# Prompt attention in a hybrid decoder step: keys of the preceding block copied over masked keys, values summed in column halves

## The chip, the cores and the metric

The kernel runs on one core of a Trainium2 chip. The metric is the device time of one execution in microseconds (us). The engines are TensorE (PE in the profile; PEld is its weight loads), VectorE (DVE), ScalarE (ACT), GpSimd (POOL) and SyncE (SP, which only issues DMAs here).

## The reference

One inference step of a two-layer decoder trunk, for a prompt (16 meta tokens and 256 prompt tokens, 272 columns) and a sample group (8 sequences of 4 tokens, 32 columns): 304 columns in all. Per layer:

```
proj = x @ w_in                       # q (8 heads x 64), k, v (2 groups x 64), xr, gate, g_attn, g_lru
attn = sliding-window attention (window 128, rotary, a learned sink per head)
rec  = RG-LRU(causal_conv(xr)) * gelu(gate)
mix  = (sigmoid(g_attn) * attn @ w_attn_proj + sigmoid(g_lru) * rec @ w_lru_proj) @ w_out
x = LayerNorm(alpha * x + mix);  x = LayerNorm(alpha * x + SwiGLU(x))
```

The prompt's attention, which the change touches, is

```
valid = (kp <= qp) & (kp > qp - 128) & (kp >= 0)      # kp, qp: positions of key and query
s = where(valid, q @ k.T / 8, -1e30);  m = max(s.max(), sink)
p = exp(s - m);  out = (p / (p.sum() + exp(sink - m))) @ v
```

So a query sees itself and the 127 positions before it. Prompt queries are cut into block 0 (the 16 meta tokens), block 1 and block 2 (128 each). For query i of a block of 128, the valid keys are keys 0 to i of its own block and keys i+1 to 127 of the block that precedes: always 128 places, one for each index.

## The kernel before, in words

Activations lie transposed, features on the partitions and the 304 tokens in the columns. Each fp32 weight block of 128x1024 is loaded by SyncE, copied by ScalarE to a rounded part (`wh`, line 212) and reduced by VectorE to the remainder (`wl`, line 213) in `prep`; every product is three matmuls in the rounded format (`product`, lines 363 to 365). `ahead` keeps these preparations `LA` = 4 units ahead of TensorE, over `WB` = 5 buffers. A product over a whole input is 24 matmuls and is called a step here.

Per layer: the grouped products for k, v and the first two q (lines 415 to 419), rotary, and then a list of steps (xr, ga, gate, gl), between which smaller work is hung by a plan written by hand (`PLAN`, `BEHIND`, lines 35 to 44): the turning of values (`v_turn`), the attention units, the convolutions, the LRU gates (lines 700 to 711) and the recurrence. Then come the attention projection, the LRU projection, the output projection with a norm and the SwiGLU.

An attention unit (`Unit`) is a pair of heads per group for one block of queries; layer 0 has one unit of block 0 and two each of blocks 1 and 2, layer 1 the latter four. Both have one `Sample` unit for the sample group. A unit has three stages:

- `scores`: a bf16 matmul of the identity with the mask (line 516) puts 0 or -8e30 in a PSUM bank, for each group; four fp32 products of K = 64 rows are added (line 521), on 144 key columns in block 1 and 256 in block 2. VectorE takes the maximum (line 527), ScalarE the exponentials with their sums (line 534), VectorE normalizes (line 540).
- `turn`: TensorE transposes the probabilities (lines 554 and, for the 16 meta keys, 558) and ScalarE copies them from PSUM (lines 560 and 563).
- `values`: products of 256 columns with the values (line 574), over value tiles that are padded with zeros so that each group writes its half of the 128 output partitions and all are added in one bank: three in block 1, four in block 2. `split` (lines 350 and 351) makes the two parts for the projection.

`BEHIND` sets how many steps lie between a unit's stages: in layer 0 turning comes three steps after scores and values one step after turning, in layer 1 four and three. The tiles of SBUF come from a pool of `SLOTS` buffers. Except in two blocks that fix an order, the framework's planner orders the instructions of each engine by the program's order and its own estimates of time, and sets the semaphores; an engine runs its list in order.

Of the kernel before, what the change touches and what calls it, by code (L numbers as in the profile page):

```python
# [122 lines left out]
def trunk_kernel(ctx, tc, I, O):  # L123
# [132 lines left out]
    mask1 = const("mask1", [128, 144], BF)  # L256
    mask2 = const("mask2", [128, 256], BF)
    mask0 = const("mask0", [16, 16], BF)
# [26 lines left out]
    dve.memset(eps, EPS)  # L285
    qblk = consts.tile([128, NB, 2, 4, NS], F32, name="qblk")
# [137 lines left out]
    for l in range(DEPTH):  # L424
# [9 lines left out]
        vt = slot(nm("vt"), [128, T])  # L434
        vz = slot(nm("vz"), [128, 2, 2, 128])
        v0 = slot(nm("v0"), [128, 2, 128])
        pool.memset(vz, 0.0)
        pool.memset(v0[:, 0], 0.0)
# [33 lines left out]
        def evac_v(ps):  # L472
            if fold is None:
                act.activation(vt, ps[:, :T], AF.Copy)
            else:
                unfold(ps, T, allc, vt)

        def v_turn():
            p = bank(nm("vT"))
            p3 = p.rearrange("p (a b) -> p a b", a=4)  # L480
            for j, (a, b) in enumerate(((0, 16), (16, 144), (144, 272), (272, 304))):
                pe.transpose(p3[:b - a, j, :], vt[:, a:b], identf)
            for g in range(2):
                d = slice(64 * g, 64 * g + 64)
                act.activation(vz[:, :, g, d], p3[:, 1:3, d], AF.Copy)
                act.activation(v0[32 * g:32 * g + 16, 0, d], p3[:16, 0, d], AF.Copy)
                pool.dma_start(O["wvp"][l][:, d], vz[:, 1, g, d])
            act.activation(v0[:32, 1, :], p3[:32, 3, :], AF.Copy)
            pool.dma_start(O["wvn"][l], v0[:32, 1, :])
# [4 lines left out]
        VN = v0[:, 1, :]  # L494
        BLK = {
            0: dict(q0=0, nq=16, keys=(0, 16), mask=mask0, first=True, v=()),
            1: dict(q0=16, nq=128, keys=(0, 144), mask=mask1, first=True, v=(0,)),
            2: dict(q0=144, nq=128, keys=(16, 272), mask=mask2, first=False, v=(0, 1)),
        }

        class Unit:

# [4 lines left out]
            def __init__(self, b, ts):  # L507
                self.B, self.ts, self.nt = BLK[b], ts, len(ts)

            def scores(self):  # L510
                B, nt = self.B, self.nt
                nq, (k0, k1) = B["nq"], B["keys"]
                nk = k1 - k0
# [12 lines left out]
                for g in range(2):  # L526
                    dve.tensor_reduce(mx[:, g], p3[g], axis=AX.X, op=OP.max)
# [595 lines left out]
```

## Time and profile before

| | us |
|---|---|
| median of 3 runs | 925.61 (922.74 to 925.91) |
| the profiled execution | 924.32 |
| its span, first to last instruction | 922.6 |
| TensorE busy | 891.0 |
| VectorE busy | 700.5 |
| ScalarE busy | 504.2 |
| GpSimd busy | 185.4 |

Times in the profile are those of the one profiled execution. Matmul ends are modelled and matmuls overlap, so the price of one is best read from the start of the next or from the chain of work that ended last, which gives to each step only the time by which it delays the next. An fp32 matmul has two records, one in bf16 or in the rounded format has one, and a transpose has one. The granted clock of TensorE is given as a share: 1.00 is 2.4 GHz, 0.50 is 1.2 GHz.

### The profile page before, as it was taken

The page shows a single profiled execution, that of the slowest core. Times are in us where ns is not written, and L with a number is a line of the kernel's source. Part 1 is how long each engine was busy: PE and PEld are TensorE (multiplying, and loading weights), DVE is VectorE, ACT ScalarE, POOL GpSimd, SP SyncE. Part 2 cuts the span into 40 slices and gives each one's busy share as a digit, 9 for nine tenths or more (in the row PEclk, how much of TensorE's full clock was granted, in tenths as well). Part 3 has the DMA queues.
Part 4 walks back from the last instruction along what each step waited for, and adds up shares of the span by engine and source line. Part 5 has one row for each costly group of instructions (what it writes and reads, how often), then busy time and mean ns, then how long its engine had stood idle before and what let it go on. Part 6 is the DMA issues. An engine that isn't in the chain of part 4 may idle for free.

```text
span 922.6 us, 16033 instructions
## 1 busy us (share of the span) xinstructions
PE 891.0 (97%) x6414; PEld 870.9 (94%) x6414; DVE 700.5 (76%) x1169; ACT 504.2 (55%) x876; POOL 185.4 (20%) x253
## 2 busy tenths in 40 slices
PE   7998999999999999999997999999999999999993
PEld 6987899999999999999997998999999999999993
DVE  5676859567998667677899888795689975877865
ACT  4864794444665334444557877963456643434432
POOL 2930219012300000000262431040252000000025
PEclk9998999999999999999998999999999999999997
DMA  7753135535345443554455253155444454445401
GB/s 247 278 193 120 53 131 184 183 138 180 140 138 180 140 161 115 185 180 138 142 213 167 91 190 112 72 181 187 163 157 152 168 175 150 144 172 183 168 16 52
DMA packets 26411, 141.61 MB, mean 153 GB/s; under 512 B 3336, under 2 KB 7464, under 8 KB 12000
## 3 DMA queue, kind: packets, MB, share of 16 engines
q1 hardware_dynamic: 25280, 137.93, 43.7%
q0 software_dynamic: 1056, 2.66, 0.9%
q8 instruction: 50, 0.82, 0.4%
q14 instruction: 25, 0.20, 0.1%
HBM read 136.74 MB, written 3.83 MB: 152 GB/s over the span
## 4 chain that ended last, share of the span: by engine, by line
PE 83%; DVE 4%; ACT 2%; issue 1%; POOL 0%; DVEq 0%; ACTq 0%
PE f L364 10%; PE f L363 10%; PE f L365 10%; PE rs L365 7%; PE rs L363 7%; PE rs L364 7%; PE gate L363 2%; PE gl L363 2%; PE rp L363 2%; PE gate L364 2%; PE rp L365 2%; PE gl L364 2%; PE rp L364 2%; PE gate L365 2%; PE gl L365 2%; PE o L574 1%
## 5 line engine op out<-in xcount | busy, mean ns | idle before, releaser
L212 ACT ACTIVATE wh<-raw 128x1024 fp32r<-128x1024 f32 (+2 forms) x255 | 263.1, 1034 | 237.1 <-PE rs L365 66.4
L213 DVE TENSOR_TENSOR wl<-raw,wh 128x1024 fp32r<-128x1024 f32 (+2 forms) x255 | 310.7, 1222 | 85.3 <-ACT wh L212 82.9
L364 PE MATMUL f<-dh,wl 128*128 128x306 f32 (+1 forms) x640 | 192.4, 301 | 0.0
L363 PE MATMUL f<-dh,wh 128*128 128x306 f32 (+1 forms) x640 | 192.2, 300 | 0.0
L365 PE MATMUL f<-dl,wh 128*128 128x306 f32 (+1 forms) x640 | 192.0, 300 | 0.0
L365 PEld LDWEIGHTS f<-dl,wh 128*128 128x128 f32 x640 | 120.7, 189 | 0.0
L364 PEld LDWEIGHTS f<-dh,wl 128*128 128x128 f32 x640 | 120.7, 189 | 0.0
L363 PEld LDWEIGHTS f<-dh,wh 128*128 128x128 f32 x640 | 120.6, 188 | 0.0
L363 PE MATMUL rs<-fh,wh 128*128 128x304 f32 (+1 forms) x352 | 105.4, 300 | 0.0
L364 PE MATMUL rs<-fh,wl 128*128 128x304 f32 (+1 forms) x352 | 104.9, 299 | 0.0
L365 PE MATMUL rs<-fl,wh 128*128 128x304 f32 (+1 forms) x352 | 104.9, 299 | 0.0
L913 POOL TENSOR_TENSOR acc<-acc,X 128x304 f32<-128x304 f32 (+1 forms) x23 | 29.7, 1290 | 359.1 <-ACT e L908 195.1
L363 PEld LDWEIGHTS rs<-fh,wh 128*128 128x128 f32 x352 | 66.3, 188 | 0.5 <-ACT fh L350 0.2
L364 PEld LDWEIGHTS rs<-fh,wl 128*128 128x128 f32 x352 | 66.2, 188 | 0.1
L365 PEld LDWEIGHTS rs<-fl,wh 128*128 128x128 f32 x352 | 66.1, 188 | 0.0
L864 DVE TENSOR_TENSOR X<-X,rs 128x304 f32<-128x304 f32 (+1 forms) x64 | 29.4, 459 | 32.2 <-PE rs L365 31.7
L363 PE MATMUL xr<-xh,wh 128*128 128x304 f32 x128 | 40.8, 319 | 4.9 <-ACT xh L791 3.9
L960 DVE SCALAR_TENSOR_TENSOR u<-c,c,f 128x304 f32<-128x304 f32 (+1 forms) x80 | 41.4, 520 | 1.8
L959 DVE COPY c<-f 128x2 f32<-128x2 f32 x80 | 12.5, 158 | 39.3 <-PE f L365 39.1
L365 PE MATMUL xr<-xl,wh 128*128 128x304 f32 x128 | 39.6, 312 | 1.6 <-DVE xl L793 1.6
L364 PE MATMUL xr<-xh,wl 128*128 128x304 f32 x128 | 39.5, 312 | 0.0
L363 PE MATMUL gate<-xh,wh 128*128 128x304 f32 (+1 forms) x128 | 39.2, 306 | 0.0
(307 smaller groups left out, 2226.1 us busy)
## 6 DMA issues: line engine op xcount, KB each, us to landing
raw<-in_wts SPq DMA_DIRECT2D x112, 1024.0 KB, 4.9
raw<-in_wts SPq DMA_DIRECT2D x16, 768.0 KB, 4.3
raw<-in_wts SPq DMA_DIRECT2D x3, 512.0 KB, 9.0
kc<-in_kcache SPq DMA_DIRECT2D x4, 256.0 KB, 7.1
vc<-in_vcache SPq DMA_DIRECT2D x4, 256.0 KB, 7.1
out_wks<-kc POOLq DMA_DIRECT2D x4, 256.0 KB, 4.9
out_wvs<-vc POOLq DMA_DIRECT2D x4, 248.0 KB, 5.1
xt<-in_xT SPq DMA_DIRECT2D x3, 304.0 KB, 8.1
```

Source lines behind the costliest of these rows:

```text
L212: act.activation(hi[:, s], r, AF.Copy)
L213: (pool if u in LO_POOL else dve).tensor_sub(lo[:, s], r, hi[:, s].bitcast(F32))
L363: pe.matmul(ps[:, :n], hi[:, w], xh, start=first, stop=False)
L364: pe.matmul(ps[:, :n], lo[:, w], xh, start=False, stop=False)
L365: pe.matmul(ps[:, :n], hi[:, w], xl, start=False, stop=last)
L574: pe.matmul(o, v, x, start=i == 0, stop=i == len(todo) - 1)
L864: dve.tensor_add(z, z, ps[:, :W])
L913: on("sum", l).tensor_add(self.sum, self.sum, z)
L959: dve.tensor_copy(c2[:, 2 * i:2 * i + 2], b[:, W:W + 2])
L960: dve.scalar_tensor_tensor(t1[:, i], off, c2[:, 2 * i + 1:2 * i + 2], b[:, :W], op0=OP.mult, op1=OP.add)
```

## The change

The scores no longer have masks added. They are made for the same key columns as before, without the mask matmul. Where a key of the query's own block lies behind the query, VectorE overwrites its score, in PSUM, with that of the key of the same index in the block that precedes (a predicated copy under `later`, an int16 triangle), or with -8e30 where there is none (columns 0 to 111 of block 1, and block 0). So every query has 128 columns, on which the maximum, the exponentials and the normalization run. `turn` makes 128-row transposes of these into one bank for both groups; then VectorE, instead of ScalarE's copy, makes two copies: times the triangle of the own keys and times that of the preceding keys (`turned`). `values` multiplies the first with the values of the own block and the second with those of the block before; each group has a product of 64 output columns, which writes its half of the partitions of the bank. The values are turned in four blocks of 128 columns behind 112 columns of zeros, so that the meta tokens are keys 112 to 127 of block 0, and need no zero padding between groups.

```diff
--- before.py
+++ after.py
@@ -253,9 +253,8 @@
-    mask1 = const("mask1", [128, 144], BF)
-    mask2 = const("mask2", [128, 256], BF)
-    mask0 = const("mask0", [16, 16], BF)
+    later = const("later", [128, 128], mybir.dt.int16)
+    turned = const("turned", [128, 2, 128])
@@ -283,6 +282,8 @@
+    big = consts.tile([128, 1], F32, name="big")
+    dve.memset(big, BIG)
@@ -431,11 +432,9 @@
-        vt = slot(nm("vt"), [128, T])
-        vz = slot(nm("vz"), [128, 2, 2, 128])
-        v0 = slot(nm("v0"), [128, 2, 128])
-        pool.memset(vz, 0.0)
-        pool.memset(v0[:, 0], 0.0)
+        vt = slot(nm("vt"), [128, 112 + T])
+        vn = slot(nm("vn"), [128, 4, 128])
+        pool.memset(vt[:, :112], 0.0)
@@ -471,107 +470,109 @@
-                act.activation(vt, ps[:, :T], AF.Copy)
+                act.activation(vt[:, 112:], ps[:, :T], AF.Copy)
             else:
-                unfold(ps, T, allc, vt)
+                unfold(ps, T, allc, vt[:, 112:])
         def v_turn():
             p = bank(nm("vT"))
             p3 = p.rearrange("p (a b) -> p a b", a=4)
-            for j, (a, b) in enumerate(((0, 16), (16, 144), (144, 272), (272, 304))):
-                pe.transpose(p3[:b - a, j, :], vt[:, a:b], identf)
-            for g in range(2):
-                d = slice(64 * g, 64 * g + 64)
-                act.activation(vz[:, :, g, d], p3[:, 1:3, d], AF.Copy)
-                act.activation(v0[32 * g:32 * g + 16, 0, d], p3[:16, 0, d], AF.Copy)
-                pool.dma_start(O["wvp"][l][:, d], vz[:, 1, g, d])
-            act.activation(v0[:32, 1, :], p3[:32, 3, :], AF.Copy)
-            pool.dma_start(O["wvn"][l], v0[:32, 1, :])
+            for j in range(4):
+                n = min(128, 112 + T - 128 * j)
+                pe.transpose(p3[:n, j, :], vt[:, 128 * j:128 * j + n], identf)
+            act.activation(vn[:, :3], p3[:, :3], AF.Copy)
+            act.activation(vn[:32, 3], p3[:32, 3], AF.Copy)
+            pool.dma_start(O["wvp"][l], vn[:, 2, :])
+            pool.dma_start(O["wvn"][l], vn[:32, 3, :])
             for j in range(2):
                 pool.dma_start(O["wvs"][l][:, 4 * j:4 * j + 4], cache["vc", j][NS:])
         attn = Split("at", T)
-        VN = v0[:, 1, :]
-        BLK = {
-            0: dict(q0=0, nq=16, keys=(0, 16), mask=mask0, first=True, v=()),
-            1: dict(q0=16, nq=128, keys=(0, 144), mask=mask1, first=True, v=(0,)),
-            2: dict(q0=144, nq=128, keys=(16, 272), mask=mask2, first=False, v=(0, 1)),
-        }
+        VN = vn[:, 3, :]
         class Unit:
             stages = ("scores", "turn", "values")
             def __init__(self, b, ts):
-                self.B, self.ts, self.nt = BLK[b], ts, len(ts)
+                self.b, self.ts, self.nt = b, ts, len(ts)
+                self.nq, self.q0 = (16, 0) if b == 0 else (128, 128 * b - 112)
             def scores(self):
-                B, nt = self.B, self.nt
-                nq, (k0, k1) = B["nq"], B["keys"]
+                b, nt, nq = self.b, self.nt, self.nq
+                k0, k1 = ((0, 16), (0, 144), (16, 272))[b]
                 nk = k1 - k0
+                own = slice(nk - nq, nk)
                 p3 = [bank(nm("sc"))[:nq, :].rearrange("p (a b) -> p a b", a=nt)[:, :, :nk] for _ in range(2)]
-                for p in p3:
-                    pe.matmul(p, identb[:nq, :nq], B["mask"][:nq, None, :].to_broadcast([nq, nt, nk]),
-                              start=True, stop=False, skip_group_check=True)
                 for a, t in enumerate(self.ts):
                     for g in range(2):
                         gs = slice(64 * g, 64 * g + 64)
-                        pe.matmul(p3[g][:, a, :], qr[t // 2][gs, t % 2, B["q0"]:B["q0"] + nq], kr[gs, k0:k1],
-                                  start=False, stop=True, skip_group_check=True)
+                        pe.matmul(p3[g][:, a, :], qr[t // 2][gs, t % 2, self.q0:self.q0 + nq], kr[gs, k0:k1],
+                                  start=True, stop=True, skip_group_check=True)
                 w = tiny("aw", 40).rearrange("p (n g t) -> p n g t", n=5, g=2)[:nq, :, :, :nt]
                 mx, neg, rs, es, rec = (w[:, n] for n in range(5))
                 sk = nsink[:nq, l, :8].rearrange("p (g t) -> p g t", g=2)[:, :, self.ts[0]:self.ts[0] + nt]
                 for g in range(2):
-                    dve.tensor_reduce(mx[:, g], p3[g], axis=AX.X, op=OP.max)
+                    p = p3[g][:, :, own]
+                    n = 128 - (0, 16, 128)[b]
+                    if n:
+                        n = min(n, nq)
+                        dve.copy_predicated(p[:, :, :n], later[:nq, None, :n].to_broadcast([nq, nt, n]),
+                                            big[:nq, None, :].to_broadcast([nq, nt, n]))
+                    if b:
+                        dve.copy_predicated(p[:, :, n:], later[:, None, n:].to_broadcast([nq, nt, 128 - n]),
+                                            p3[g][:, :, :128 - n])
+                    dve.tensor_reduce(mx[:, g], p, axis=AX.X, op=OP.max)
                 dve.scalar_tensor_tensor(neg, mx, -0.125, sk, op0=OP.mult, op1=OP.min)
                 dve.tensor_sub(es, neg, sk)
                 act.activation(es, es, AF.Exp)
-                self.P = [slot(nm("P"), [128, nt, nk]) for _ in range(2)]
+                self.P = [slot(nm("P"), [128, nt, 128]) for _ in range(2)]
                 for g in range(2):
+                    P = self.P[g][:nq]
+                    if b == 0:
+                        pool.memset(P[:, :, :112], 0.0)
                     for a in range(nt):
-                        act.activation(self.P[g][:nq, a, :], p3[g][:, a, :], AF.Exp, bias=neg[:, g, a:a + 1],
+                        act.activation(P[:, a, 128 - nq:], p3[g][:, a, own], AF.Exp, bias=neg[:, g, a:a + 1],
                                        scale=0.125, accum_out=rs[:, g, a:a + 1])
                 dve.tensor_add(es, es, rs)
                 dve.reciprocal(rec, es)
                 for g in range(2):
-                    P = self.P[g][:nq]
-                    dve.tensor_mul(P, P, rec[:, g, :, None].to_broadcast([nq, nt, nk]))
+                    P = self.P[g][:nq, :, 128 - nq:]
+                    dve.tensor_mul(P, P, rec[:, g, :, None].to_broadcast([nq, nt, nq]))
             def turn(self):
-                B, nt = self.B, self.nt
-                nq, nf, nv = B["nq"], 16 * B["first"], len(B["v"])
+                nt, nq = self.nt, self.nq
+                n = 2 * nt * nq
+                p = bank(nm("pt"))
+                for g in range(2):
+                    for a in range(nt):
+                        i = (g * nt + a) * nq
+                        pe.transpose(p[:, i:i + nq], self.P[g][:nq, a, :], identf[:nq, :nq])
+                if self.b == 0:
+                    x = slot(nm("PT"), [128, n])
+                    act.activation(x, p[:, :n], AF.Copy)
+                    self.PT = [(0, x)]
+                else:
+                    self.PT = []
+                    for i in range(2):
+                        x = slot(nm("PT"), [128, n])
+                        dve.tensor_mul(x.rearrange("p (a b) -> p a b", a=4), p.rearrange("p (a b) -> p a b", a=4),
+                                       turned[:, i, None, :].to_broadcast([128, 4, 128]))
+                        self.PT.append((self.b - i, x))
+            def values(self):
+                nt, nq, q0 = self.nt, self.nq, self.q0
                 n = nt * nq
-                if nf:
-                    self.F = slot(nm("PF"), [128, n])
-                    pool.memset(self.F[:48], 0.0)
-                self.PT = []
-                for g in range(2):
-                    p = bank(nm("pt"))
-                    for j in range(nv):
-                        for a in range(nt):
-                            pe.transpose(p[:, j * n + a * nq:j * n + (a + 1) * nq],
-                                         self.P[g][:nq, a, nf + 128 * j:nf + 128 * (j + 1)], identf[:nq, :nq])
-                    if nf:
-                        for a in range(nt):
-                            pe.transpose(p[:16, nv * n + a * nq:nv * n + (a + 1) * nq], self.P[g][:nq, a, :16],
-                                         identf[:nq, :nq])
-                        act.activation(self.F[32 * g:32 * g + 16], p[:16, nv * n:(nv + 1) * n], AF.Copy)
-                    if nv:
-                        x = slot(nm("PT"), [128, nv, n])
-                        act.activation(x, p[:, :nv * n].rearrange("p (a b) -> p a b", a=nv), AF.Copy)
-                        self.PT.append(x)
-            def values(self):
-                B, nt = self.B, self.nt
-                nq, q0 = B["nq"], B["q0"]
-                o = bank(nm("o"))[:, :nt * nq]
-                todo = [(vz[:, v, g, :], self.PT[g][:, j]) for j, v in enumerate(B["v"]) for g in range(2)]
-                if B["first"]:
-                    todo.append((v0[:48, 0, :], self.F[:48]))
-                for i, (v, x) in enumerate(todo):
-                    pe.matmul(o, v, x, start=i == 0, stop=i == len(todo) - 1)
+                o = bank(nm("o"))[:, :n]
+                for i, (v, x) in enumerate(self.PT):
+                    for g in range(2):
+                        gs = slice(64 * g, 64 * g + 64)
+                        pe.matmul(o[gs, :], vn[:, v, gs], x[:, g * n:(g + 1) * n], start=i == 0,
+                                  stop=i == len(self.PT) - 1, skip_group_check=True)
@@ -1048,10 +1049,7 @@
-    c0 = np.arange(16)[None, :]
-    mask1 = np.concatenate([m(c0 > q - 112), m(k <= q)], 1)
-    mask2 = np.concatenate([m(k > q), m(k <= q)], 1)
-    mask0 = m(c0 <= np.arange(16)[:, None])
+    turned = np.stack([q <= k, q > k], 1).astype(np.float32)
@@ -1061,7 +1059,7 @@
-                mask1=mask1, mask2=mask2, mask0=mask0, masks=np.stack(ms, 1))
+                later=(k > q).astype(np.int16), turned=turned, masks=np.stack(ms, 1))
```

## Rows read from the trace of the kernel before

**Rows 1.** The page's busy times of the whole span, with shares and instructions.

```profile
PE 891.0 (97%) x6414; PEld 870.9 (94%) x6414; DVE 700.5 (76%) x1169; ACT 504.2 (55%) x876; POOL 185.4 (20%) x253
```

**Rows 2.** Windows: stretch, its length, busy time (instructions) of each engine, clock, DMA share, GB/s.

```profile
60.00:120.00 60.00, 55.13 (x370) 48.27 (x359) 45.73 (x99) 39.29 (x103) 8.41 (x16) 0.94 0.33 111
...
520.00:620.00 100.00, 98.49 (x734) 93.44 (x732) 81.92 (x154) 79.07 (x175) 28.00 (x37) 1.00 0.38 126
```

**Rows 3.** Waits of TensorE, layer 1: total us, times, longest.

```profile
PE rg L700 <- ACT xch L350: 1.5, 1, 1.5
```

**Rows 4.** Timeline of TensorE, layer 0: start, us, operation, [idle before, releaser].

```profile
69.10 0.70 PE L574 MATMUL o<-PT,vz 128*128 128x256 f32 x2 [1.06 <-ACT PT L563]
...
82.40 1.17 PE L627 MATMUL so<-v,sPT 32*128 32x128 f32 x4 [2.91 <-ACT sPT L621]
...
99.41 0.70 PE L574 MATMUL o<-PT,vz 128*128 128x256 f32 x2 [0.32 <-ACT PT L563]
...
114.01 0.70 PE L574 MATMUL o<-PT,vz 128*128 128x256 f32 x2 [0.57 <-ACT PT L563]
```

**Rows 5.** Windows around the longest of these waits, columns as in rows 2.

```profile
79.40:82.40 3.00, 0.09 (x2) 0.00 (x1) 2.37 (x4) 2.83 (x7) 0.00 (x0) 1.00 0.68 240
...
82.40:85.50 3.10, 3.10 (x24) 1.62 (x24) 0.92 (x3) 0.25 (x1) 0.00 (x0) 0.51 0.68 209
...
85.50:88.70 3.20, 3.20 (x13) 2.38 (x13) 1.11 (x2) 0.00 (x0) 0.00 (x0) 0.50 0.35 146
```

**Rows 6.** Timeline of ScalarE in the first of these stretches.

```profile
79.57 1.06 ACT L212 ACTIVATE wh<-raw 128x1024 fp32r<-128x1024 f32 x1 [1.51 <-PE ga L365]
...
81.99 0.36 ACT L621 ACTIVATE sPT<-spt 32x256 f32<-32x256 f32 x1
```

**Rows 7.** Chain of work that ended last, layer 1: start, us, step.

```profile
529.74 0.26 PE sc L516 x2
...
532.79 0.22 PE pt L558 x2
...
562.45 1.49 PE o L574 x6
...
563.94 0.54 PE sc L516 x2
...
564.48 1.06 PE sc L521 x8
...
582.40 0.57 PE so L631 x16
...
586.38 0.87 PE pt L554 x8
...
597.02 1.73 PE o L574 x8
```

**Rows 8.** Groups of VectorE by shape: count, busy us, mean ns, idle before.

```profile
L213 DVE TENSOR_TENSOR wl<-raw,wh 128x1024 fp32r<-128x1024 f32 x233 | 291.5, 1254 | 75.4 <-ACT wh L212 73.2
...
L540 DVE TENSOR_TENSOR P<-P,aw 128x512 f32<-128x512 f32 x8 | 5.2, 685 | 0.1
...
L540 DVE TENSOR_TENSOR P<-P,aw 128x288 f32<-128x288 f32 x8 | 3.4, 465 | 0.1
...
L351 DVE TENSOR_TENSOR atl<-o,ath 128x256 fp32r<-128x256 f32 x8 | 3.4, 420 | 1.7 <-ACT ath L350 1.6
...
L351 DVE TENSOR_TENSOR atl<-o,ath 128x32 fp32r<-128x32 f32 x2 | 0.4, 184 | 0.0
...
L685 DVE SCALAR_TENSOR_TENSOR xc<-ext,cvec,xc 128x328 f32<-128x328 f32 x48 | 25.8, 558 | 2.4 <-POOL xc L683 2.3
```

**Rows 9.** The same for ScalarE.

```profile
L563 ACT ACTIVATE PT<-pt 128x512 f32<-128x512 f32 x8 | 4.4, 590 | 0.0
...
L563 ACT ACTIVATE PT<-pt 128x256 f32<-128x256 f32 x8 | 3.0, 370 | 0.0
...
L560 ACT ACTIVATE PF<-pt 16x256 f32<-16x256 f32 x8 | 2.9, 365 | 0.1
```

## The prediction

> **What bounds the kernel now.** I read the busy times of the page first, then the windows over the stretches with attention, then what TensorE waited for, then the chain of work that ended last. TensorE is busy 891.0 us of a span of 922.6 [rows 1]. So a microsecond of matmul time taken from a stretch where it runs without gaps should come off the end, and one of another engine should not, unless it makes TensorE wait. The change lies in two stretches: in layer 0 from about 40 to 130 us, in layer 1 from about 520 to 620 us. They differ. Layer 0 from 60 to 120 us leaves TensorE idle for 60 - 55.13 = 4.9 us; layer 1's 100 us only for 1.5 us [rows 2], nearly all of it one wait of the LRU gates for the convolution's split [rows 3]. VectorE is busy 45.73 of 60 us in the first and 81.92 of 100 in the second [rows 2].
>
> In layer 0 the idle time is four waits ahead of value products: 1.06, 0.32 and 0.57 us for a unit's copied turned probabilities, and 2.91 us for those of the sample group [rows 4]. The last one is dear: TensorE's granted clock was 1.00 through the idle stretch, then 0.51 and 0.50 from 82.4 to 88.7 us (the 1.2 GHz level), in which it was busy all the time [rows 5]. Work of 6.3 us at half clock would take 3.15 us at full, so that wait costs 2.9 + 3.15 = 6.05 us. Its cause is the order on ScalarE: the copies of the sample's turned probabilities end at 82.35 us, behind a weight copy that could begin only at 79.57, when TensorE had finished a product and released a buffer [rows 6].
>
> **What comes off TensorE.** The steps of the chain at full clock are the prices [rows 7]. I count one layer: two units of block 1 and two of block 2.
> - Mask matmuls go: 0.26 us for the pair of a block 1 unit and 0.54 us for that of block 2. 2 x 0.26 + 2 x 0.54 = 1.60 us.
> - Turning: a block 2 unit has 8 transposes in 0.87 us and keeps 4; a block 1 unit loses its four narrow ones at 0.11 us each (two took 0.22). 2 x 0.44 + 2 x 0.44 = 1.75 us.
> - Values: block 2 has four full-width products in 1.73 us, block 1 three in 1.49 us. Both become four products with 64 output columns, in two pairs that write different halves of the partitions. No row shows such a pair. The bounds: one after the other they cost what four full products cost, 1.73 us; side by side they cost what the scores of block 2 do, four products on half the array with the same 256 columns, two at a time: 1.06 us. I take 1.06, because the sample's value products, which write quarters of the partitions, show 8 matmuls (16 records) of 128 columns in 0.57 us [rows 7]. A full product of 256 columns costs 1.73 / 4 = 0.43, so 8 of 128 in a row would cost 1.7. Saved: 2 x (1.73 - 1.06) + 2 x (1.49 - 1.06) = 2.20 us.
>
> Sum 5.55 us in a layer, 11.1 in both. Block 0's unit loses two tiny mask products and gets wider weights in its eight transposes, some tenths each way: nothing. With the value products in a row the 4.4 us of both layers go, and block 1's four units lose 0.24 each: 11.1 - 4.4 - 1.0 = 5.7.
>
> The trace speaks here about one rule that is against the change. The sample's quarters all use the same rows of the array and yet ran three times as fast as in a row [rows 7]. The Trainium skill, "TensorE: Matmul & The Clock Gate", Part 3, says that a weight load overlaps matmuls in flight only where the row group differs, and the two halves share it. By that rule the pairs would hide less and the saving would lie nearer to 5.7; the trace does not bear it out for quarters, and halves are not in it.
>
> **What is added on VectorE.** Durations by shape [rows 8]. The predicated copies are in no row. I price them by the tensor_tensor that reads PSUM, 0.42 us at 256 columns and 0.18 at 32. Below, 0.18 each, the shortest of these rows; above, I allow two passes, twice my price.
> - Block 1 unit: per group one copy of 224 and one of 32 columns, 0.39 + 0.18 (0.39 lies between the two rows), for two groups 1.1 us. Two products with the triangles, 512 columns from PSUM: 2 x 0.69 = 1.4. Two normalizations go from 288 columns (0.465) to 256 (0.42), and two reductions, taken at the same price: -0.2. Net +2.3 us.
> - Block 2 unit: copies 2 x 0.42 = 0.84, triangles +1.4, reductions and normalizations from 512 columns (0.69 each) to 256 (0.42): 4 x -0.27 = -1.1. Net +1.1 us.
>
> A layer: 2 x 2.3 + 2 x 1.1 = 6.8 us, 13.6 in all (up to 13.6 + 2 x (2 x 1.1 + 2 x 0.84) = 21.4 with two passes), on 700.5. ScalarE loses the copies: per block 1 unit 2 x 0.37 and 2 x 0.365, per block 2 unit 2 x 0.59 [rows 9], 5.3 us a layer, and block 2's exponentials get half as wide. The sums on both engines hide behind TensorE as long as the order leaves room. In layer 1 there are four steps of 24 matmuls between scores and turning and three between turning and values, 10 us or more each, and weights are made ahead, so I cost it at nothing there. If that cover went, each value wait would cost what it does in layer 0.
>
> **What moves in layer 0.** There, values follow turning by one step. The wait for the copy goes from ScalarE to VectorE. The first value pair now needs a product of 0.69 us instead of a copy of 0.37 or 0.59, over all eight transposed blocks: +0.2 on the mean; the second pair needs the next 0.69, of which the first pair covers 0.53: +0.15. VectorE is also fuller, and its weight remainder of 1.25 us [rows 8] is the commonest thing to stand in front: half of one, +0.6. That is 0.95 us for each of four units, 3.8 us. The bounds: -1.95, if the three waits vanish, and a wait of 2.9 us with its half clock for each unit (below). What is queued behind the triangles on VectorE are convolutions and weight remainders; the gates wait for the former and TensorE's next products for the latter, four units ahead.
>
> Small edits at nothing: three constants of 100 KB become two of 160 KB on the same queue, behind the first weights; one zero tile fewer on GpSimd; one store of values instead of two on its queue; three copies fewer in the turning of values on ScalarE; one memset at the start on VectorE. Each lies beside busy matmuls or before the layer's waits. Values get 112 more columns of zeros, which cost no further transpose.
>
> **Sum.** The profiled execution took 924.3 us, between the runs (922.74 to 925.91, median 925.61), so I use it without a correction: 924.3 - 11.1 + 3.8 = 917.0 us, with the long sample wait left where it is.
>
> **Rivals.**
> 1. The sample wait goes. The order on each engine is the planner's, worked out from its own estimates, and every unit's work changes; if the sample's copies come ahead of the weight copy, 6.05 us more come off: 911 us. For it: ScalarE has fewer copies in that stretch. Against: what the copies stood behind, a buffer that TensorE had to release, does not change.
> 2. Another wait of that kind comes in, anywhere in layer 0's dense stretch or at a gate: one more wait near 2.9 us with its half clock, 917 + 6 = 923 us. For it: every unit of layer 0 has one step of room there, and VectorE is fuller. Against: three of the four waits of that kind were 1.06 us or less [rows 4].
> 3. The halves don't run side by side: 924.3 - 5.7 + 3.8 = 922 us. Against it are the quarters.
> 4. Slower: VectorE becomes the engine that sets layer 0. In 60 to 120 us it has 14.3 us free and gets up to 6.8 more while the stretch is to shrink by 5.5. If the triangles queue behind a convolution (three steps of 0.56 us, and its split) and a weight remainder, the wait ahead of a unit's values is about 3 us, and half clock follows as it did once: 6 us a unit. Three units give 924.3 - 11.1 + 18 = 931, four give 937. I put it at 934. It decides against the change from a mean wait of 11.1 / 4 = 2.8 us a unit, or half that where the clock falls too. Against it: a good part of VectorE's free time in that stretch is waiting for the slow TensorE, and work can move behind 120 us.
>
> **How the numbers follow.** A half per cent, 4.6 us, is about what a measurement of this kernel can tell from no change. The forecast has 0.38, the sample wait gone 0.22, another wait 0.16, halves in a row 0.08, VectorE 0.16. Faster (under 921 us): 0.38 + 0.22 = 0.60. Same: 0.16 + 0.08 = 0.24. Slower: 0.16. Range: from 907 us (sample wait gone and the small ones with it) to 928 us (another wait, and copies of two passes); it leaves out most of rival 4 and a little at the bottom.
>
> **What would show it.** After, the mask lines are gone; the turning takes 0.43 us a unit in the chain; the value products of a unit take near 1.06 us (1.73 says rival 3). The predicated copies take 0.2 to 0.4 us for 32 to 256 columns. The value products in layer 0 wait for the VectorE multiply, about 1 to 1.5 us each; the sample's value products wait 2.9 us and a stretch at half clock follows, or neither. Layer 1 keeps TensorE busy within 2 us of its span. The forecast is wrong if VectorE in layer 0 is busy above nine tenths and the clock falls more than once there.

## The result and the profile after

The changed kernel took 913.58 us in the median (912.34 to 914.91); the kernel before, beside it, 924.89. The ratio is 0.9892, with a 95% interval of 0.9872 to 0.9912: 11.3 us less. The forecast was 917 us in a range of 907 to 928. The profiled execution after took 914.91 us with a span of 912.8, so the spans differ by 9.8 us.

First the busy times of the page after, as in [rows 1]:

```profile
PE 884.9 (97%) x6374; PEld 864.6 (95%) x6374; DVE 711.4 (78%) x1212; ACT 493.0 (54%) x845; POOL 182.4 (20%) x246
```

TensorE has 6.1 us less, VectorE 10.9 us more (the forecast said 13.6), ScalarE 11.2 us less (10.6). The busy time of TensorE shows less than the 11.1 us of matmuls that were to go. Ahead of layer 0's first xr product it is 2.1 us more (33.2 against 31.1), in a stretch that moves between runs of one program (e5_again below), and in layer 0 matmuls at half clock count longer.

The two dense stretches, columns as in [rows 2] (the second is 110 us long here):

```profile
60.00:120.00 60.00, 53.81 (x353) 47.49 (x352) 48.92 (x112) 35.85 (x92) 7.78 (x10) 0.91 0.33 117
...
510.00:620.00 110.00, 108.87 (x824) 103.10 (x824) 98.47 (x189) 83.73 (x180) 31.56 (x42) 1.00 0.44 147
```

and what TensorE waited for: in layer 0, then (last row) in layer 1, as in [rows 3, 4], with total, times and the longest:

```profile
PE o L574 <- DVE PT L563: 3.3, 2, 1.7
...
PE so L628 <- ACT sPT L622: 2.9, 1, 2.9
...
PE rg L701 <- ACT xch L351: 0.9, 2, 0.6
```

Layer 1 is idle for 1.1 us in 110. Layer 0 is idle for 6.2 us in 60, where it was 4.9, and its granted clock is 0.91 on the mean. The sample group's wait is there again with its 2.9 us. The waits for ScalarE's copies (1.95 us) are replaced by two for VectorE's multiplied copies, 3.3 us.

The prices on TensorE, from the chain of work that ended last in layer 1, as in [rows 7]:

```profile
525.17 0.69 PE sc L514 x8
...
527.75 0.44 PE pt L554 x4
...
539.56 1.01 PE o L574 x8
...
601.48 1.01 PE o L574 x8
```

Scores of block 1 cost 0.69 us without a mask in front, the four transposes of a unit 0.44, the value products 1.01 in block 1 (539.56) and block 2 (601.48) alike. And VectorE's prices by shape, as in [rows 8]:

```profile
L563 DVE TENSOR_TENSOR PT<-pt,turned 128x512 f32<-128x512 f32 x16 | 10.6, 682 | 0.1
...
L524 DVE COPY_PREDICATED_SCALAR sc<-later,big 128x224 f32 x8 | 3.2, 441 | 0.0
...
L527 DVE COPY_PREDICATED sc<-later,sc 128x256 f32<-128x256 int16 x8 | 3.1, 427 | 2.8 <-PE sc L514 2.8
...
L527 DVE COPY_PREDICATED sc<-later,sc 128x32 f32<-128x32 int16 x8 | 1.2, 186 | 0.0
```

The predicated copies, which no row of before showed, cost 0.43 us at 256 columns and 0.19 at 32, almost what the tensor_tensor of the same width does [rows 8], and 0.44 at 224 with a constant as the source.

Where the 9.8 us come off can be read from the first starts of products in both traces: the products of xr and of the attention projection (ap), layer 0 then layer 1, of the kernel before,

```profile
L363 PE MATMUL xr<-xh,wh x64: 299/304/408, 36.0 to 67.5; 128*128 128x304 f32 x64
...
L363 PE MATMUL ap<-ath,wh x32: 297/302/305, 173.9 to 186.8; 128*128 128x304 f32 x32
...
L363 PE MATMUL xr<-xh,wh x64: 299/302/455, 497.6 to 532.0; 128*128 128x304 f32 x64
...
L363 PE MATMUL ap<-ath,wh x32: 292/295/298, 628.2 to 640.5; 128*128 128x288 f32 x32
```

and of the kernel after (columns: count, duration in ns, first and last start in us):

```profile
L364 PE MATMUL xr<-xh,wh x64: 299/303/409, 35.1 to 65.9; 128*128 128x304 f32 x64
...
L364 PE MATMUL ap<-ath,wh x32: 296/300/305, 171.2 to 184.1; 128*128 128x304 f32 x32
...
L364 PE MATMUL xr<-xh,wh x64: 296/303/455, 493.8 to 527.2; 128*128 128x304 f32 x64
...
L364 PE MATMUL ap<-ath,wh x32: 291/295/297, 618.4 to 630.7; 128*128 128x288 f32 x32
```

To the first xr product of layer 0, 0.9 us (35.1 against 36.0). From there to layer 0's first ap product, the stretch that holds its attention, 1.8 us (136.1 against 137.9). From there to layer 1's first xr product 1.1 us (322.6 against 323.7). In layer 1 from the first xr to the first ap product 6.0 us (124.6 against 130.6). Behind that, nothing (294.4 to the end of both). So layer 1 gained 6.0 us for its 5.55 us of matmuls, and layer 0 a third of them.

Layer 1's part can be read more closely from its first scores to its first ap product, before and then after, columns as in [rows 2]:

```profile
515.60:628.20 112.60, 110.12 (x821) 104.58 (x820) 91.44 (x167) 86.80 (x187) 30.44 (x42) 1.00 0.40 136
...
511.60:618.40 106.80, 105.67 (x801) 100.08 (x801) 96.83 (x187) 80.83 (x174) 29.96 (x40) 1.00 0.42 143
```

Of these 5.8 us, 4.45 are busy time and 1.35 idle time. Counted from each start to the next, value products, masks and transposes take 5.7 us less, as the forecast had it. But the scores of the first unit are now split by a wait of 0.2 us for VectorE (before, a wait of 1.0 us stood behind them) and take 0.6 us more, and the gates and steps around them take another 0.6 us more, which was not followed. That the sum comes so near to the count is in part luck.

Layer 0 once more, in windows from the sample wait on, columns as in [rows 5]:

```profile
77.00:80.90 3.90, 0.99 (x8) 0.74 (x7) 3.89 (x7) 3.00 (x8) 0.00 (x0) 1.00 0.39 118
...
80.90:84.00 3.10, 3.10 (x26) 2.29 (x28) 0.89 (x3) 0.22 (x1) 0.00 (x0) 0.56 0.86 290
...
84.00:86.00 2.00, 2.00 (x13) 1.35 (x11) 1.19 (x4) 0.00 (x0) 0.00 (x0) 0.83 0.57 238
...
92.00:96.60 4.60, 3.04 (x23) 2.82 (x21) 4.51 (x12) 3.81 (x12) 0.00 (x0) 1.00 0.11 16
...
96.60:100.00 3.40, 3.40 (x16) 1.86 (x16) 3.37 (x7) 2.01 (x4) 1.81 (x1) 0.75 0.77 289
...
100.00:102.00 2.00, 2.00 (x8) 1.61 (x7) 1.18 (x4) 0.39 (x1) 0.00 (x0) 0.50 0.00 0
...
102.00:104.00 2.00, 2.00 (x10) 2.00 (x9) 1.00 (x3) 1.68 (x4) 0.54 (x1) 0.50 0.00 0
...
104.00:106.00 2.00, 2.00 (x12) 2.00 (x12) 2.00 (x7) 1.88 (x10) 0.00 (x0) 0.71 0.00 0
```

TensorE was idle for 2.9 of the first 3.9 us, and the clock fell behind it as before, for a shorter time: from about 81 to 84.5 us, against 6.3 us in [rows 5]. But then comes a second fall: the stretch 92 to 96.6 us holds a wait of 1.56 us for a multiplied copy, and from 98 to 105 us the clock is at half (1.2 GHz), although TensorE was busy throughout. What the clock and the waits take in 60 to 120 us, as idle time and (1 - clock) x 60: 4.9 + 3.6 = 8.5 us before, 6.2 + 5.4 = 11.6 us after. Of layer 0's 5.55 us of matmuls, 3.1 went there.

The sample wait has the cause that was read from [rows 6]: its copies (ending at 80.8) stand on ScalarE behind a weight copy that waited for TensorE to finish a product.

```profile
78.04 1.06 ACT L212 ACTIVATE wh<-raw 128x1024 fp32r<-128x1024 f32 x1 [0.90 <-PE ga L366]
...
80.46 0.36 ACT L622 ACTIVATE sPT<-spt 32x256 f32<-32x256 f32 x1
```

### The profile page after: what moved, and what is told of

Its sections match the earlier page's. It is cut to its first block, busy times and chain, and to the rows that moved or that the text cites. A ratio compares the mean times of both kernels' runs of the same rounds, so it can differ in the third digit from the quotient of the medians.

```text
span 912.8 us, 15955 instructions
## 1 busy us (share of the span) xinstructions
PE 884.9 (97%) x6374; PEld 864.6 (95%) x6374; DVE 711.4 (78%) x1212; ACT 493.0 (54%) x845; POOL 182.4 (20%) x246
## 4 chain that ended last, share of the span: by engine, by line
PE 84%; DVE 7%; ACT 3%; POOL 3%; DMA 2%; issue 1%; SPq 0%; DVEq 0%; ACTq 0%; POOLq 0%
PE f L365 10%; PE f L366 10%; PE f L364 10%; PE rs L364 7%; PE rs L366 7%; PE rs L365 7%; PE gl L364 2%; PE rp L366 2%; PE gl L365 2%; PE rp L364 2%; PE rp L365 2%; PE gl L366 2%; PE gate L364 2%; PE gate L366 2%; PE gate L365 2%; DVE wl L213 1%
```

## The experiments

The theory: the matmuls are worth what the chain says (11.1 us); layer 1 gets them in full; layer 0 gives part back, because each wait ahead of value products comes with one step of room, and two of the waits pull the clock down. Its rivals: the halves or masks were hidden anyway; VectorE's added work sets the end; the waits belong to the engines' orders and go elsewhere when they are moved.

Medians are compared as ratios with the runs of the kernel before beside them. The stretches are from the first xr to the first ap product of each layer, in us, and show where a difference lies; the last column is layer 1 from its first scores to its first ap product:

| kernel | median us | ratio to before (95%) | layer 0 | layer 1 | layer 1 from its scores |
|---|---|---|---|---|---|
| before | 924.89 | 1 | 137.9 | 130.6 | 112.6 |
| after | 913.58 | 0.9892 (0.9872 to 0.9912) | 136.1 | 124.6 | 106.8 |
| e5_again (after, unedited) | 912.68 | 0.9900 (0.9885 to 0.9915) | 135.1 | 123.5 | 106.8 |
| e1_full | 923.63 | 1.0013 (0.9999 to 1.0027) | 138.8 | 127.6 | 109.3 |
| e2_masks | 916.20 | 0.9928 (0.9905 to 0.9951) | 134.8 | 126.4 | 108.3 |
| e3_twice | 918.18 | 0.9955 (0.9938 to 0.9971) | 137.9 | 124.5 | 107.2 |
| e10_halves (on before) | 919.37 | 0.9960 (0.9945 to 0.9975) | 138.0 | 128.7 | 111.0 |
| e11_copies | 913.18 | 0.9893 (0.9879 to 0.9908) | 134.1 | 125.3 | 107.4 |
| e4_later | 908.27 | 0.9851 (0.9827 to 0.9876) | 129.5 | 124.9 | 106.9 |
| e6_sample | 914.09 | 0.9914 (0.9899 to 0.9928) | 135.0 | 124.3 | 106.8 |
| e7_units | 908.46 | 0.9849 (0.9833 to 0.9865) | 129.8 | 124.1 | 106.8 |
| e8_before_later (on before) | 916.68 | 0.9939 (0.9923 to 0.9956) | 131.4 | 129.4 | 112.7 |
| e9_back | 907.35 | 0.9829 (0.9814 to 0.9845) | 129.2 | 124.9 | 106.9 |

**The changed kernel again.**

> The changed kernel once more, unedited, beside the next three on one chip: the yardstick for spans and stretches. Ratio to the kernel before 0.987 to 0.991. If TensorE's idle time in the first 25 us moves by up to 3 us between runs of one program, it differs from the first trace's 1.9 us; if that is fixed by the program, it doesn't. The waits of layer 0 (2.9 us for the sample group's copies, 1.6 to 1.7 us for two multiplied copies) and the two stretches at half clock should be there again.

The intervals overlap. The stretches moved by 1.0 and 1.1 us between two profiled executions of one program, and TensorE's busy time in the first 25 us by 1.7 us (23.08 and 21.35). So a stretch of one trace is good to about 1 us, and the start is no property of an edit. In layer 1 all of that lies ahead of the first scores (17.8 and 16.7 us from the first xr product to them). From there on both traces take 106.8 us, and so does every variant of the changed kernel below that leaves layer 1 alone, within 0.1 us. The sample's wait was 2.9 us again, the waits for multiplied copies 3.8 us in three, and two falls of the clock followed. Idle time and half clock in 60 to 120 us make 6.7 + 3.6 = 10.3 us here, 1.8 more than before the change, where the first trace has 3.1 more.

**Halves undone.**

```diff
-    pe.matmul(o[gs, :], vn[:, v, gs], x[:, g * n:(g + 1) * n], start=i == 0, ...)
+    z = vz[:, v - 1, g, :] if v else v0[:, g, :]      # zero-padded to 128 columns
+    pe.matmul(o, z, x[:, g * n:(g + 1) * n], start=i == 0 and g == 0, ...)
```

> Undoes the halves: the value products have 128 output columns again, over zero-padded values; all else as in the changed kernel. If the halves run side by side, as its trace's 1.01 us a unit says against 1.73 for four full products in the kernel before, TensorE gets 0.72 us more in each of eight units, 5.8 us in all: 913.6 + 5.8 = 919.4 us, with nearly 2.9 us of it in layer 1. If the halves gain nothing (they only look overlapped in the records): 913.6, within 1 us.

One of the four units of layer 1 in the chain of this kernel, a wait of TensorE in layer 0, and ScalarE before it:

```profile
545.27 1.73 PE o L582 x8
...
PE o L582 <- ACT PT L565: 2.7, 1, 2.7
...
50.97 0.40 ACT L677 ACTIVATE ext<-xr 128x272 f32<-128x272 f32 x1 [5.64 <-POOL ext L674]
```

Every unit takes 1.73 us again, against 1.01: the halves run side by side. Layer 1 is 3.0 us longer (4.1 over the second run of after, and 2.5 from the first scores on), where 2.9 was counted. The median lost 11 us (0.0121 x 923), more than the 5.8. In layer 0 there is a new wait of 2.7 us for the copy of block 0's unit. The order of ScalarE's work ahead of that copy is as in the changed kernel, but ScalarE came to it late: it had waited 5.64 us for GpSimd's `ext` (last row; 1.4 us in the changed kernel), which stood on GpSimd behind small preparations (`spw`) that ended at 50.7 us, where in the changed kernel they ended at 34.1. So part of the 11 us is not the price of the halves. What the rest of the gap is was not settled; the edit also zeroes and fills two more value tiles.

**Halves alone, on the kernel before.**

```diff
-    pe.matmul(o, v, x, start=i == 0, stop=i == len(todo) - 1)
+    for g in range(2):
+        gs = slice(64 * g, 64 * g + 64)
+        v, x = j(g, gs)                               # columns gs of the same tiles
+        pe.matmul(o[gs, :], v, x, start=i == 0, stop=i == len(jobs) - 1, ...)
```

> The kernel before with one part of the change alone: its value products, the padded one of the meta keys too, are made as halves of 64 output columns; masks, transposes and ScalarE's copies stay. Theory: a block 2 unit takes 1.0 us instead of 1.73, a block 1 unit 1.0 instead of 1.49, so layer 1 gets 2.4 us shorter and layer 0 the same if its waits stay: 922.3 - 4.8 = 917.5 us. Rival (layer 0's waits and half clock change with the order and hide it): layer 1 by 2.4 us all the same, layer 0 by anything from -5 to +3.

Chain in layer 1 (block 1, block 2), then from layer 0 the first value product with its wait, the window behind it, and 60 to 120 us as a whole:

```profile
544.20 1.16 PE o L577 x8
...
595.79 1.01 PE o L577 x8
...
69.13 0.65 PE L577 MATMUL o<-PT,vz 128*64 128x256 f32 x2 [1.06 <-ACT PT L563]
...
71.00:75.00 4.00, 4.00 (x21) 3.50 (x20) 3.75 (x9) 1.59 (x9) 0.12 (x1) 0.57 0.48 190
...
60.00:120.00 60.00, 54.45 (x369) 46.32 (x358) 46.08 (x98) 39.40 (x104) 9.57 (x15) 0.94 0.32 106
```

Layer 1 gains 1.9 us (0.72 in each block 2 unit, 0.33 in block 1's, which has the odd 48-row product: 2.1 by the chain, and 1.6 from the first scores on). Layer 0 gains nothing in this trace, 138.0 against 137.9. Behind the same wait of 1.06 us as in [rows 4], at the same place, the clock now falls to half, between 71 and 75 us. In the kernel before, whose products there have the full width, it stayed up:

```profile
69.00:73.00 4.00, 3.90 (x22) 2.56 (x23) 2.10 (x4) 2.22 (x6) 0.79 (x2) 1.00 0.67 227
```

But the clock is not what took the gain: its mean over 60 to 120 us is 0.94 in both kernels, since the fall behind the sample wait is shorter here. The idle time is 0.7 us more (5.55 against 4.87); the rest was not located. The profiled execution is also the slowest of six (917.73 to 921.68). The median gained 0.0040 x 923 = 3.7 us (2.3 to 5.1) of the 4.8 counted. So the halves gain by themselves; whether layer 0 hides its part of them, as the rival has it, stays undecided.

**Masks put back.**

```diff
+    for p in p3:
+        pe.matmul(p, identb[:nq, :nq], zmask[:nq, None, :].to_broadcast([nq, nt, nk]), start=True, stop=False, ...)
-    pe.matmul(p3[g][:, a, :], ..., start=True, stop=True, ...)
+    pe.matmul(p3[g][:, a, :], ..., start=False, stop=True, ...)
```

> The changed kernel with the mask matmuls put back in front of the scores, of zeros, so that they cost their time and change no value. Theory: their 1.60 us a layer comes back in full in layer 1 and about so in layer 0: 913.6 + 3.2 to 4 = 917 us. Rival (they hid in gaps and the gain came from elsewhere): 913.6, within 1 us.

Chain in layer 1, then from layer 0 a value product with its wait for a multiplied copy, and the window with it and the one behind:

```profile
525.60 0.26 PE sc L514 x2
...
558.04 0.54 PE sc L514 x2
...
97.68 0.65 PE L579 MATMUL o<-PT,vn 128*64 128x256 f32 x4 [1.58 <-DVE PT L568]
...
96.00:100.00 4.00, 2.42 (x17) 1.11 (x18) 3.88 (x8) 3.37 (x8) 1.02 (x1) 1.00 0.63 199
...
100.00:104.00 4.00, 4.00 (x31) 3.67 (x28) 3.91 (x12) 2.58 (x9) 1.33 (x2) 1.00 0.16 66
```

The masks cost 0.26 and 0.54 us as in [rows 7], and layer 1 is 1.8 us longer (1.5 from the first scores on), 1.6 counted. Layer 0 is not longer: 134.8 us, against 136.1 and 135.1 in the two runs of after. What can offset the masks there is in the windows: the wait of 1.58 us is still there, yet the clock stays at 1.00 behind it. The median lost 0.0036 x 923 = 3.3 us, as forecast for both layers; the traces put only part of that into the two stretches.

**Predicated copies twice.**

```diff
+    for _ in range(2):
         if n: dve.copy_predicated(p[:, :, :n], ...)
         if b: dve.copy_predicated(p[:, :, n:], ...)
```

> Each predicated copy is done twice, the second time to no effect: 1.25 us more VectorE work in a block 1 unit, 0.85 in a block 2 unit, 4.2 us a layer. Theory: layer 1 hides it and layer 0 has three steps between scores and turning: 913.6 to 915 us. Rival (VectorE sets the end in the dense stretches): at least 4 us in layer 0 and some in layer 1, 918 to 922 us.

TensorE's wait for the multiplied copies in layer 0:

```profile
PE o L575 <- DVE PT L564: 6.5, 3, 3.7
```

Layer 1 hides the work but for 0.4 us (107.2 from its first scores on, for 106.8). Layer 0 does not: its waits for multiplied copies go from 3.3 or 3.8 us to 6.5, one of them 3.7, and the stretch is 1.8 to 2.8 us longer. The median lost 0.0063 x 923 = 5.8 us, within the rival's range, though the rival had at least 4 us of it in layer 0. Here my theory was wrong on layer 0: VectorE's added work has little cover there. The stretch shows less than the median. The profiled execution was the fastest of its six (916.77, where the median is 918.18); where the rest lies was not settled.

**Triangles left out, copies on ScalarE.**

```diff
-    dve.tensor_mul(x.rearrange(...), p.rearrange(...), turned[:, i, None, :].to_broadcast([128, 4, 128]))
+    act.activation(x, p[:, :n], AF.Copy)
```

> Leaves out the two triangles: the turned probabilities are copied twice by ScalarE, without the product that separates own from preceding keys, so the values are summed over too much. VectorE loses 1.3 us a unit, ScalarE gets 1.1. If VectorE's queue is what the value products of layer 0 wait for (3.3 to 3.8 us and a half clock behind them), layer 0 gets 2 to 5 us shorter: 908 to 911 us. If one step is too short whichever engine makes the copies, as the 1.95 us of the kernel before on ScalarE suggest, layer 0 changes by less than 1.5 us: 911 to 914 us.

```profile
PE o L573 <- ACT PT L563: 2.5, 2, 2.1
```

This is TensorE's wait in layer 0. 2.5 us in place of 3.3 or 3.8, the median the same as after's, the stretch 1 to 2 us shorter. So it is not much VectorE against ScalarE: one step is too short for either.

**Values one step later in layer 0: all, the sample group alone, the other units alone.**

```diff
-BEHIND = ((0, 3, 4, 5), (0, 4, 7, 9))
+BEHIND = ((0, 3, 5, 6), (0, 4, 7, 9))
```

This is e4_later. In e6_sample the units keep (0, 3, 4) in layer 0 and the sample group has (0, 3, 5, 6); in e7_units the units have (0, 3, 5) and the sample group keeps (0, 3, 4, 5).

> One size changed: in layer 0 the value products come two steps after the turning instead of one (sample group included, its last stage one later too). Theory: what layer 0 lost went to the waits ahead of value products (6.2 us idle) and to the half clock behind two of them (5.0 us): most of 11 us comes off, 903 to 906 us. Rival (the waits belong to the order of ScalarE and VectorE and turn up at other places, or the convolutions set them): 912 to 915 us.

> In layer 0 the sample group's values come one step later, the other units' don't. Theory: its wait of 2.9 us goes and the half clock behind it (about 3.6 us at half, 1.8 lost): layer 0 gets 4.7 us shorter, 909 us. Rival (the wait only moves, as the planner keeps the weight copy ahead of the sample's copies): layer 0 within 1.5 us, 913 us.

> In layer 0 the other units' values come one step later, the sample group's don't. Theory: the two waits for VectorE's multiplied copies go (3.3 us) and the half clock behind the second (6.5 us at half, 3.2 lost): layer 0 gets up to 6.5 us shorter, 907 us. Rival (these waits were small change, the sample wait with its clock is what layer 0 loses): layer 0 by at most 3.3 us, 910 to 912 us.

Layer 0's window of 60 to 120 us, each followed by the longest wait in that stretch, for all (e4_later):

```profile
60.00:120.00 60.00, 55.95 (x412) 50.50 (x412) 51.11 (x118) 40.22 (x102) 8.18 (x15) 0.97 0.34 117
...
PE sot L640 <- DVE sO L635: 4.0, 1, 4.0
```

for the sample group alone (e6_sample):

```profile
60.00:120.00 60.00, 54.26 (x360) 47.23 (x360) 50.62 (x114) 37.12 (x96) 6.49 (x10) 0.91 0.35 117
...
PE sot L641 <- DVE sO L636: 4.1, 1, 4.1
```

and for the other units alone (e7_units):

```profile
60.00:120.00 60.00, 56.82 (x404) 51.48 (x397) 52.07 (x118) 39.77 (x100) 8.97 (x15) 0.94 0.34 117
...
PE so L629 <- ACT sPT L623: 3.2, 1, 3.2
```

All moved, the median is 908.3 us, short of the 903 to 906 expected, with a new wait of 4.0 us. Moving the other units alone takes 5.3 to 6.3 us off layer 0 (4.0 and 4.7 us in the median, over the two sets of runs of after), the whole gain of moving all: their waits are gone, the second half clock with them, and the sample's wait (3.2 us) with its half clock stays. Moving the sample alone brings nothing: its wait goes from the values to the step behind (`sot`, 4.1 us for a VectorE product), and the clock is at 0.91 as before. So the rival held for the sample group and the theory for the units. My price of the sample wait, 6.05 us, is idle time and clock read from one trace, and one more step does not bring it: the wait moves on.

**The same step on the kernel before.**

```diff
-BEHIND = ((0, 3, 4, 5), (0, 4, 7, 9))
+BEHIND = ((0, 3, 5, 6), (0, 4, 7, 9))
```

> The kernel before, with layer 0's values (sample group included) one step later. If the later step is worth what the kernel before lost there, 4.9 us idle and 3.15 us of half clock, it gets up to 8 us faster, 0.991 to 0.993 of the kernel before, and the change is then worth 11.1 us over it, as counted in matmuls. If the later step helps only the changed kernel, 0.998 to 1.002.

```profile
60.00:120.00 60.00, 57.76 (x419) 52.52 (x419) 47.03 (x101) 45.89 (x114) 9.18 (x17) 1.00 0.34 117
```

That is its layer 0 window: 2.2 us idle and the clock at 1.00 from end to end. It gains 6.5 us there (4.9 + 3.6 - 2.2 = 6.3 by idle time and clock) and 0.0061 x 922 = 5.6 us in the median, short of the 0.991 to 0.993 expected. On top of it the change is worth 0.9851 / 0.9939, 0.9 per cent or 8 us (e4_later; 5 to 11 with both intervals), not the 11.1 expected: 4.5 us in layer 1 (129.4 to 124.9), and in layer 0 only 1.9 of 5.55, since the changed kernel still has a wait of 4 us and a half clock there.

**A version that beats both.** Values later for the units and the sample, and the sample's last stage one more.

```diff
-BEHIND = ((0, 3, 4, 5), (0, 4, 7, 9))
+BEHIND = ((0, 3, 5), (0, 4, 7))
+SAMPLE = ((0, 3, 5, 7), (0, 4, 7, 9))
```

> The changed kernel with layer 0's values two steps after the turning for all units, as in the run with all values later, and the sample group's last stage two steps after its values instead of one. That run lost in layer 0 one wait of 4.0 us for the sample's VectorE product and some 1.7 us of half clock behind it. Theory: both go, 908.3 - 5 = 903 us. Rival (the wait turns up at the next thing of the sample group): 907 to 909 us.

```profile
60.00:120.00 60.00, 57.04 (x404) 51.65 (x404) 51.22 (x115) 43.24 (x104) 8.21 (x11) 0.97 0.38 130
...
PE rg L702 <- ACT tg L757: 2.0, 2, 1.7
```

0.9829 of the kernel before is the best ratio here, though its interval overlaps those of e4_later and e7_units. The wait for `sot` went, and others came: the gates for a tanh copy, 2.0 us in two (second row), with the clock at 0.97 on the mean (first row). That is the rival: 907.4, not 903.

## Why the prediction was right

The direction, the size and the place were right; the sum of 917 was 3.4 us too high, and the range held. In two terms the sum came out near by other ways than it said, which is luck.

- Matmuls taken off, 5.55 us a layer: right in its prices. Transposes 0.44 us a unit (forecast 0.43; no run puts them back, so this rests on the chain alone), value products 1.01 (1.06, taken from the scores on half the array), masks 0.26 and 0.54 when put back. Layer 1 gained 6.0 us in the first trace and 7.1 in the second, and 5.8 in both from its first scores on: 4.45 of busy time, and 1.35 of waits that the sum did not have. The forecast's window for layer 1, 520 to 620 us, begins behind the first scores (515.6 us) and so left out the wait of 1.0 us behind them.
- The halves side by side: right, shown by undoing them (1.73) and by doing them alone (1.01). The Trainium skill, "TensorE: Matmul & The Clock Gate", Part 3, has weight loads overlap matmuls in flight only where the row group differs. The two halves share the row group and a pair costs little more than one full product (1.01 / 2 against 0.43), so the trace does not agree with a price that follows from it. Nor does it agree with the rule for full products: after the change, weight loads were busy for 864.6 us and matmuls for 884.9 us of the same 912.8, nearly all of them on all 128 rows.
- VectorE's work: 10.9 us for 13.6. The copies came at 0.44, 0.43 and 0.19 for the 0.39, 0.42 and 0.18 assumed, the triangles at 0.68. By durations the sum is 14.5 us; the engine's busy time grew by less, because neighbours on it overlap. Layer 1 hid it, as said, and nearly all of twice the copies too.
- Layer 0's added waits, 3.8 us: near in size in the first trace (3.1 us by idle time and clock, and 5.55 - 1.8 = 3.7 by the stretch), too high in the second (1.8 and 2.8), and not right in kind. I had four waits that grow by a little under a microsecond each. In the first trace there were two that are long, 1.3 us more idle time in all, and the rest, about 1.8 us, was a second fall of the clock behind a wait of 1.56 us. In the second trace there were three waits, 1.8 us more idle time in all, and the two falls cost no more than the one before the change did. My sum had no second fall, and of a fall behind a shorter wait than 2.9 us I spoke only in rival 4's condition. So it was the forecast's sum with a piece of rival 2 in it. Of my sign of being wrong, one half came: the clock fell twice in layer 0, but VectorE was busy for 48.92 of 60 us, 0.82.
- The term that the sum held at nothing and the first traces do not is what lies outside the two stretches: 0.9 us before layer 0's attention and 1.1 us between it and layer 1's. The forecast's 7.3 us, these 2.0 and layer 1's surplus of 0.45 make the 9.8 us by which the spans differ. The 0.9 is no more than the start moves: layer 0's first xr product comes at 35.1 and 35.5 us in the two traces of after, and at 34.8 to 37.7 in its variants. Of the 1.1, 0.8 is TensorE's wait for ScalarE's copy of layer 1's input (`xh`), 3.9 us before and 3.1 after. The 1.1 showed again in e5_again (322.5 from the first ap to layer 1's first xr product), but the variants of the changed kernel have 322.0 to 323.8 there and the kernel before and its variants 323.2 to 323.7, so it is not shown to belong to the change. The medians differ by 11.3 us, 1.5 more than the spans; the profiled execution after was the slowest of its four, and the second trace has a span of 911.1.
- Rival 1 (the sample wait goes) did not happen: the order on ScalarE that makes it stayed. Rival 3 (halves in a row) was refuted. Rival 4 (VectorE) did not happen. With 4.2 us more of VectorE work a layer, e3_twice lost 5.8 us, with a wait of 3.7 us in layer 0, and was still faster than the kernel before (0.9955).

## What to carry to other kernels

Take the price of a matmul from the chain at full clock and from its nearest relative in shape, and it holds where the engine has few gaps (layer 1); where the same work has one step between a producer and a consumer, a shorter matmul stage gives much of its gain back as waits. When an edit takes work off TensorE in such a stretch, look first for a handover that can be given another step: that was worth 5 to 6.5 us of layer 0 (4 to 5.6 us of the median) on either kernel, as much as the whole change in that layer should have been. And a wait that is moved need not go: the sample group's went to its next stage, and from there to the gates.

## What the runs showed of the hardware

Two fp32 products that use all 128 rows and either half of the output columns ran side by side: a unit of four, with 256 columns each, took 1.01 us in the chain, and four at full width 1.73 us.

The clock fell to 1.2 GHz behind waits shorter than I had thought, and not in the order of their length. Behind a wait of 1.06 us with halves after it, it was 0.57 (71 to 75 us of e10_halves); behind the same wait with full-width products after it, 1.00 (69 to 73 us of the kernel before). But behind 0.99 us in the same run of e10_halves, at 100 us and again with halves after it, it stayed at 1.00. In layer 0 of the changed kernel it fell behind the wait of 1.56 us (98 to 105 us) and not behind the one of 1.71 us (68 to 72 us); e2_masks stayed at 1.00 behind 1.58 us, and e8_before_later behind 2.24 us (95 to 99 us). Each of these is one execution. Why one wait and not the other stays open, since the granted clock of these stretches is all that the traces show.

The predicated copy, scores from PSUM to PSUM under a triangle of int16, costs about what a plain two-operand pass of that width costs: 0.43 against 0.42 us at 256 columns, and 0.19 against 0.18 at 32. With a constant as its source it took 0.44 us at 224 columns.
